# Constant matmuls in planned TensorE gaps, and longer DMA times in the planner of a hybrid decoder layer

## The chip, the cores and the metric

One core of one Trainium2 chip runs the whole program. The metric is device microseconds (us) of one execution; the time before is the median of three runs.

## What is computed

One layer of a hybrid decoder on a prompt of 2048 tokens (plus 16 meta tokens) and on 8 short sampled sequences of 4 tokens. The reference, cut down:

```python
h = rmsnorm(x, ln1_w)
p = einsum('btd,de->bte', h, w_in)          # one wide projection, 1024 -> 10384
# branch A: causal conv + SiLU on q/k/v, then the gated delta rule in chunks of 64,
#           8 heads of 128x128 state
# branch B: token shift, LoRA decays, RWKV-7 state update, 16 heads of 64x64 state
merged = sigmoid(gA) * (oA @ w_out_a) + sigmoid(gB) * (oB @ w_out_b)
x_new = x + merged @ w_out
y = rmsnorm(x_new, lnf_w)                   # and the new states of both branches
```

## The kernel before, in words

The tokens are cut into five segments of 6 or 7 chunks of 64 (368 to 448 columns). Of each segment the kernel computes the normalised, transposed input (`hHL`, a high and a low fp32r half), then twelve units: four pairs of heads of branch A (kind G) and eight of branch B (kind R), then the sixteen gate tiles, then three closing projections (kind f). A unit begins with projections (stage P, tiles `ps_p`): for each 128 columns of a weight, `proj` (L974) takes two halves of the weight, each split into `wh` and `wl`, and runs 12 fp32r matmuls on each. Then come the conv and other elementwise work, the inversion of the chunk matrices (`iM`, `iT`, `iD`, with small transfers through DRAM: `ex`, `bk`, `Dn`, `Dt`; stage M), and the recurrence over chunks (stage C, small fp32 matmuls in `ps_c`, `ps_n`, `ps_g`). An fp32 matmul shows as four rows of MATMUL and four of LDWEIGHTS in the profile, an fp32r matmul as one of each.

All of this is first recorded and not issued. `Rec.add` (L302) makes a node of each operation, and `Rec.cost` (L346) gives it a duration and a latency: for a DMA 0.07 us on its queue and 2.1 us until it has landed. `Sched.run` (L700) then simulates the five engines with these costs and so fixes the order of every engine's instructions; `replay` (L866) issues them in that order. On the chip the engines wait for each other's data by semaphores and each runs its own list strictly in order. All DMAs are issued on the one queue of SyncE (SP).

What matters for the change in the planner:

- `pick_pe` (L812) chooses the next matmul node of TensorE among the ready ones; where it has none it returns nothing, and the plan leaves TensorE idle. `clock` (L797) lets the plan run TensorE at half speed after a stretch of its own clock in which it planned under 3000 columns.
- `can` (L541), `take` (L576) and `drop` (L586) book buffers. Weight tiles (tag `w`, ten slots of 256 KB) are taken in the order of the list `worder`; a slot is free as soon as its last planned reader is done.
- PSUM has eight banks by tag: two each of `p`, `a` and `c`, one each of `n` and `g`.

Planned costs of fp32 matmuls with 128 moving columns, by the formulas of L353 to L356: 213 ns for a stationary operand of 128x128 (mode F), 134 ns for 64x128 (C), 110 ns for 128x64 (B), 86 ns for 64x64 (A). Small products are recorded in pairs or fours on different quarters of the array, and the formulas count one of such a set.

Of the kernel before, what the change touches and what calls it, by code (L numbers as in the profile page):

```python
# [16 lines left out]
C = 64  # L17
# [229 lines left out]
class Rec:  # L247
# [98 lines left out]
    def cost(s, n, e, name, a, k, outs, ins, mode):  # L346
        f = lambda x: prod(x.shape[1:])
        if e == "PE":
            n.cols += (128 if name == "transpose" else f(a[2])) * (1 if name == "transpose" or a[1].dtype == F32R else 2)
            if name == "transpose":  # L350
                n.dur += 0.107
            elif a[1].dtype == F32R:
                n.dur += (f(a[2]) / 2.4 + 14.5) / 1000  # L353
            else:
                N = f(a[2])
                n.dur += {"A": max(54, 54 + 0.5 * (N - 64)), "B": max(56, 0.86 * N), "C": max(70, 1.05 * N), "F": max(110, 4 * N / 2.4)}[mode] / 1000  # L356
            n.lat = 0.18 if a[1].dtype == F32R else 0.27
        elif e == "SP":
            o = outs[0] if outs else a[0]
            by = prod(o.shape) * 4  # L360
            last = lambda x: x.ap[-1][1] * 4 if x.ap[-1][0] == 1 else 4
            ap = [y.ap_ if isinstance(y, V) else y for y in (a[0], a[1])]
            seg = min(last(y) for y in ap)
            nd = by / max(seg, 4)
            n.kb = max(by, nd * 256)
            n.dur, n.lat = 0.07, 2.1
        else:
            N = max(f(x) for x in outs[:1] + ins[:1]) if outs else 0
            ps = any((isinstance(x, V) and x.root.psum) for x in ins)
            if e == "DVE":  # L370
                d = N / 0.96 + 160
                if name == "scalar_tensor_tensor":
                    d += 40
                if name == "tensor_tensor_scan":
                    d = 2 * N / 0.96 + 160
            elif e == "ACT":
                d = 0.82 * N + (165 if ps else 240)
            else:
                d = {"tensor_tensor": 2.35 * N + 100, "memset": 0.6 * N + 80}.get(name, 1.1 * N + 150)
            n.dur += d / 1000  # L380
            n.lat = 0.09
        if e == "PE":
            return
# [63 lines left out]
class Sched:  # L447
# [93 lines left out]
    def can(s, n):  # L541
        need = {}
        for r in n.allocs:
            k = (r.pool, r.tag)
            need[k] = need.get(k, 0) + 1
        u = n.unit
        for k, c in need.items():
            av = len(s.free[k]) - c
            if av < 0:
                return False  # L550
            if k[1] == "w":
                if not s.worder or s.worder[0] is not n:
                    return False
                continue
            if k[0].space == PSUM:
                continue
            L = u.seqs[k]
            i = u.idx[k]
            if L[i] is not n.allocs[[(r.pool, r.tag) for r in n.allocs].index(k)]:
                return False  # L560
            for v in s.active:
                if v.age > u.age:
                    break
                if k not in v.idx:
                    continue
                h, j = v.held[k], v.idx[k]
                if v is u:
                    h, j = h + c, j + c
                if max(0, v.peak[k][j] - h) > av:
                    return False  # L570
                av += h
            if u not in s.active and max(0, u.peak[k][i + c] - c) > av:
                return False
        return True
# [11 lines left out]
    def drop(s, r):  # L586
        k = (r.pool, r.tag)
        s.free[k].append(r.slot)
        if k in r.unit.held and not r.psum and r.tag != "w":
            r.unit.held[k] -= 1  # L590

# [108 lines left out]
    def run(s):  # L700
# [2 lines left out]
        E = ["PE", "DVE", "ACT", "POOL", "SP"]  # L703
        s.rdy = {e: [] for e in E}
        s.active, s.worder, s.pq, s.cur, s.infl, s.wpend = [], [], [], None, [], []
        s.lastunit, s.late = s.porder["last"], s.porder["late"]
        tfree = dict.fromkeys(E, 0.0)
        s.mode, s.burst = "F", 0
# [12 lines left out]
        while done < total:  # L721
            s.commit()
            prog = True
            while prog:
                prog = False
                for e in E:
                    if tfree[e] > s.now + 1e-9:
                        continue
                    n = s.pick_pe() if e == "PE" else s.pick(e)
                    if n is None:  # L730
                        continue
                    prog = True
                    d = n.dur
                    if e == "PE":
                        if n.mode != s.mode:
                            d += s.SWITCH
                            s.stat["sw"] += 1
                        s.clock()
                        if s.half:
                            d *= 2  # L740
                        w0, w1 = int(s.now / 3.4133), int((s.now + d) / 3.4133)
                        for w in range(w0, w1 + 1):
                            part = min((w + 1) * 3.4133, s.now + d) - max(w * 3.4133, s.now)
                            s.cols[w] = s.cols.get(w, 0) + n.cols * part / d
                        s.mode = n.mode
                        isP = n.pt is not None and len(n.ops) * 2 > PG
                        s.burst = s.burst + 1 if isP else (s.burst if n.mode == "F" else 0)
                        s.stat["P" if isP else "s"] += n.dur
                        s.stat["idle"] += s.now - max(tfree[e], 0)
                        if n.pt is not None and n is n.pt.pe[-1]:  # L750
                            s.pq.remove(n.pt)
                    else:
                        s.rdy[e].remove(n)
                    s.take(n)
                    n.started, n.start = True, s.now
                    s.on_started(n)
                    out.append(n)
                    nstart += 1
                    tfree[e] = s.now + d
                    fin = s.now + d + n.lat  # L760
                    if e == "SP":
                        dma = max(dma, s.now) + n.kb / 330e3
                        fin = max(fin, dma + n.lat)
                    c += 1
                    heapq.heappush(ev, (tfree[e], c, None))
                    c += 1
                    heapq.heappush(ev, (fin, c, n))
                    if e == "PE":
                        s.commit()
            if not ev:  # L770
                self_dump(s)
                raise RuntimeError("stuck")
            t, _, n = heapq.heappop(ev)
            s.now = max(s.now, t)
            L = [n]
            while ev and ev[0][0] <= s.now + 1e-9:
                L.append(heapq.heappop(ev)[2])
            for n in L:
                if n is None:
                    continue  # L780
                done += 1
                n.unit.left -= 1
                if n.unit.left == 0:
                    s.active.remove(n.unit)
                for r in n.roots:
                    r.left -= 1
                    if r.left == 0:
                        s.drop(r)
                for m in n.succ:
                    m.nd -= 1  # L790
                    m.rt = s.now
                    if m.nd == 0 and m.en and not (m.pt is not None and m.eng == "PE"):
                        s.rdy[m.eng].append(m)
        s.order = out
        return out

    def clock(s):  # L797
        w = int(s.now / 3.4133)
# [62 lines left out]


BCH, BMX, BVL, AGE, ZUR = 4, 16, 3.0, 0.1, 0.5


def replay(tc, rec, order):  # L866
# [11 lines left out]
class Trunk:  # L878
# [117 lines left out]
    def setup(self):  # L996
        nc, I = self.nc, self.I
        P = self.p_c
        nc.scalar.preload_act_table_set("natural_log_exp_and_others")
        self.eps = P.tile([128, 4], F32, name="eps")  # L1000
        nc.vector.memset(self.eps[:, 0:1], EPS)
        nc.vector.memset(self.eps[:, 1:2], GN_EPS)
        nc.vector.memset(self.eps[:, 2:3], 1.0)
        nc.vector.memset(self.eps[:, 3:4], -2.4260151319598084)
        self.consts = P.tile([128, CONST_ON], F32, name="consts")
        nc.sync.dma_start(self.consts[:, 0:128], I["consts"][:, 0:128])

    def g_setup(self):
        nc, I = self.nc, self.I
# [1303 lines left out]
```

## Time and profile before

| | |
|---|---|
| median of 3 runs | 4490.87 us (4485.87 to 4494.15) |
| the profiled execution | 4488.34 us, of which its span is 4486.6 us |
| mean granted clock of TensorE | 0.936 of 2.4 GHz |
| TensorE matmul busy | 4138.6 us, 92% of the span |
| VectorE, ScalarE, GpSimd busy | 2725.4, 1973.8 and 984.4 us |
| moved by DMA | 790.08 MB |

PE is the matmul row of TensorE, PEld its weight loads, DVE VectorE, ACT ScalarE, POOL GpSimd, SPq the issuing of DMAs by SyncE. Almost every instruction has line 875, that of `replay`, so groups are told apart by the names of their tiles. PEclk is the clock that TensorE was granted: 1.00 is 2.4 GHz, 0.50 is 1.2 GHz.

### The profile page before, as it was taken

The page shows a single profiled execution, that of the slowest core. Times are in us where ns is not written, and L with a number is a line of the kernel's source. Part 1 is how long each engine was busy: PE and PEld are TensorE (multiplying, and loading weights), DVE is VectorE, ACT ScalarE, POOL GpSimd, SP SyncE. Part 2 cuts the span into 40 slices and gives each one's busy share as a digit, 9 for nine tenths or more (in the row PEclk, how much of TensorE's full clock was granted, in tenths as well). Part 3 has the DMA queues.
Part 4 walks back from the last instruction along what each step waited for, and adds up shares of the span by engine and source line. Part 5 has one row for each costly group of instructions (what it writes and reads, how often), then busy time and mean ns, then how long its engine had stood idle before and what let it go on. Part 6 is the DMA issues. An engine that isn't in the chain of part 4 may idle for free. (4 is left out here: it accounts for less than half of the span.)

```text
span 4486.6 us, 91248 instructions
## 1 busy us (share of the span) xinstructions
PE 4138.6 (92%) x32684; PEld 3467.9 (77%) x32684; DVE 2725.4 (61%) x7052; ACT 1973.8 (44%) x4842; POOL 984.4 (22%) x1972
## 2 busy tenths in 40 slices
PE   6788999998999999998999999999999999989997
PEld 6677777777878788877777787878777888768776
DVE  5877766756666554556667544676654547656642
ACT  5444543434445344444444442545444434544431
POOL 3333333323122121112212121121122102211210
PEclk9887898899999899999999999999999999999998
DMA  7544665659645456754445576544446865444457
GB/s 253 179 139 139 194 222 173 193 192 306 189 130 164 126 175 214 248 175 121 138 125 150 166 238 212 178 127 144 135 135 183 258 192 174 137 122 131 142 181 241
DMA packets 660687, 790.08 MB, mean 176 GB/s; under 512 B 251105, under 2 KB 347209, under 8 KB 660234
## 3 DMA queue, kind: packets, MB, share of 16 engines
q1 hardware_dynamic: 660234, 784.25, 56.5%
q8 instruction: 259, 4.24, 0.4%
q14 instruction: 194, 1.59, 0.1%
HBM read 602.29 MB, written 180.56 MB: 174 GB/s over the span
## 5 line engine op out<-in xcount | busy, mean ns | idle before, releaser
L875 PE MATMUL ps_p<-hHL,wh 128*128 128x448 f32 (+3 forms) x7760 | 1938.3, 378 | 39.2 <-DMA wh<-wh 20.3
L875 PEld LDWEIGHTS ps_p<-hHL,wh 128*128 128x128 f32 x7760 | 1395.4, 195 | 186.6 <-issue 62.7
L875 PE MATMUL ps_p<-hHL,wl 128*128 128x448 f32 (+3 forms) x3880 | 910.1, 357 | 1.5 <-DVE wl L875 1.0
L875 PEld LDWEIGHTS ps_p<-hHL,wl 128*128 128x128 f32 x3880 | 727.8, 193 | 36.8 <-DVE wl L875 1.6
L875 POOL COPY xo<-X 64x64 f32<-64x64 f32 x528 | 177.4, 336 | 819.5 <-ACT X L875 445.2
L875 DVE TENSOR_TENSOR iT<-iM,iD 56x1 f32<-56x1 f32 (+1 forms) x900 | 293.2, 326 | 72.4 <-DMA iD<-in_consts 54.7
L875 ACT COPY raw<-ps_p 128x448 f32<-128x448 f32 (+3 forms) x285 | 144.0, 505 | 341.2 <-PE ps_p L875 316.2
L875 DVE SCALAR_TENSOR_TENSOR cv<-raw,pv,cv 128x448 f32<-128x448 f32 (+1 forms) x360 | 261.1, 725 | 37.0 <-ACT cv L875 28.1
L875 DVE TENSOR_REDUCE iD<-iT 56x1 f32<-56x1 f32 (+1 forms) x900 | 205.1, 228 | 17.6
L875 POOL TENSOR_TENSOR wl<-wr,wh 128x512 fp32r<-128x512 f32 x105 | 146.4, 1394 | 218.7 <-ACT wh L875 101.9
L875 ACT ACTIVATE X<-ps_c,dc 64x64 f32<-64x64 f32 x224 | 69.0, 309 | 266.7 <-DVE X L875 153.4
L875 ACT CAST wh<-wr 128x512 fp32r<-128x512 f32 x210 | 129.3, 616 | 114.5 <-PE ps_p L875 36.2
L875 ACT ACTIVATE X<-ps_c 64x64 f32<-64x64 f32 x264 | 54.3, 216 | 261.7 <-DVE X L875 134.9
L875 DVE SCALAR_TENSOR_TENSOR gs<-gs,gl,ps_g 128x128 f32<-128x128 f32 x264 | 84.5, 344 | 125.2 <-PE ps_g L875 86.8
L875 POOL TENSOR_TENSOR Nt<-AL,consts 64x448 f32<-64x448 f32 (+1 forms) x80 | 93.7, 1171 | 292.9 <-DVE AL L875 288.4
L875 PE MATMUL ps_p<-mhl,wh 128*128 128x448 f32 (+2 forms) x640 | 156.1, 371 | 0.6 <-DMA wh<-wh 0.4
L875 ACT ACTIVATE sig<-cv 128x448 f32<-128x448 f32 (+2 forms) x120 | 67.4, 561 | 185.6 <-DVE cv L875 184.3
L875 PE MATMUL ps_g<-gs,cv 128*64 128x128 f32 x1056 | 122.1, 307 | 25.7 <-DVE wbd L875 9.6
L875 DVE TENSOR_SCALAR X<-ps_c,dc 64x64 f32<-64x64 f32 x224 | 65.1, 291 | 128.2 <-PE ps_c L875 83.8
L875 PEld LDWEIGHTS ps_n<-Z,Wp 64*64 64x64 f32 x3168 | 113.2, 146 | 34.5 <-DVE Z L875 15.4
L875 PE MATMUL ps_n<-Z,Wp 64*64 64x16 f32 (+1 forms) x3168 | 123.1, 222 | 12.4 <-DVE Z L875 12.1
L875 DVE TENSOR_TENSOR Z<-Dt,ps_n 128x336 f32<-128x336 f32 (+1 forms) x180 | 67.0, 372 | 101.7 <-PE ps_n L875 84.2
(337 smaller groups left out, 7483.4 us busy)
## 6 DMA issues: line engine op xcount, KB each, us to landing
wh<-wh SPq DMA_DIRECT2D x1050, 256.0 KB
wl<-wl SPq DMA_DIRECT2D x1050, 256.0 KB
wr<-in_wt SPq DMA_DIRECT2D x210, 256.0 KB
gl<-gt SPq DMA_DIRECT2D x72, 224.0 KB
gt<-gt SPq DMA_DIRECT2D x48, 224.0 KB
xt<-in_x_prompt SPq DMA_DIRECT2D x29, 256.0 KB
xt<-in_x_prompt SPq DMA_DIRECT2D x13, 512.0 KB
out_y_p<-xt SPq DMA_DIRECT2D x26, 256.0 KB
```

Source lines behind the costliest of these rows:

```text
L875: getattr(getattr(nc, eng), name)(*[g(x) for x in a], **{q: g(x) for q, x in k.items()})
```

## The change

Three things change, all of them in the planner.

- Where `pick_pe` has nothing, the planned time is past 60 us and projections are still to come, `keep` may place a matmul of constants: 128 columns of `consts` against a stationary operand of `consts`, in the mode of the last matmul, written to the first free PSUM bank in the order `n`, `a`, `g`, `c`, `p`. It does so while the present stretch of the plan has under 4500 columns (it counts as 256). Nobody reads the result. The bank is booked for its duration and 0.2 us more.
- DMAs that are not loads or stores of weights count as landing after 3.0 us and not 2.1.
- A weight slot is taken again at the earliest 1.0 us after its last planned reader is done.

```diff
-            n.dur, n.lat = 0.07, 2.1
+            n.dur, n.lat = 0.07, WLAT if n.stage == "W" else DLAT
...
-                if not s.worder or s.worder[0] is not n:
+                if not s.worder or s.worder[0] is not n or (WMAR and s.freed.get(s.free[k][0], 0) > s.now - WMAR):
                     return False
...
         s.free[k].append(r.slot)
+        if r.tag == "w":
+            s.freed[r.slot] = s.now
+            if WMAR:
+                s.wake.append(s.now + WMAR + 0.001)
...
                     n = s.pick_pe() if e == "PE" else s.pick(e)
+                    if n is None and e == "PE" and s.now > KT0 and (len(s.porder["unit"]) or s.pq):
+                        n = s.keep()
...
+    def keep(s):
+
+        w = int(s.now / 3.4133)
+        if s.cols.get(w, 0) + (s.cols.get(w - 1, 0) if False else 0) >= KEEP or (w + 1) * 3.4133 - s.now < 0.2:
+            return None
+        for tag in "nagcp":
+            k = next((k for k in s.free if k[1] == tag and k[0].space == PSUM), None)
+            if k and s.free[k]:
+                break
+        else:
+            return None
+        r = Root(k[0], tag, [128, 512], F32, "keep", None)
+        r.psum, r.left = True, 1
+        r.unit = s.nounit
+        n = Node(-1, "PE", None, "P")
+        m = n.mode = s.mode
+        K, M = (64 if m in "AC" else 128), (64 if m in "AB" else 128)
+        c = s.rec.consts
+        n.ops = [("tensor", "matmul", (V(r, None, (("__getitem__", ((slice(0, M), slice(0, 128)),), {}),)), c[0:K, 0:M], c[0:K, 0:128]), dict(start=True, stop=True))]
+        n.dur = {"A": 86, "B": 110, "C": 134, "F": 213}[m] / 1000
+        n.lat, n.cols, n.roots, n.allocs = 0.2, 256, [r], [r]
+        return n
...
+WLAT, DLAT, WMAR = 2.1, 3.0, 1.0
+KEEP, KT0 = 4500, 60.0
...
+        nc.consts = self.consts
```

## Rows read from the trace of the kernel before

**Rows 1.** Cores: span and mean granted clock

```profile
core 0: 4486.6 us, clock 0.936
```

**Rows 2.** The page: TensorE's busy time, and its clock in 40 slices

```profile
PE 4138.6 (92%) x32684; PEld 3467.9 (77%) x32684; DVE 2725.4 (61%) x7052; ACT 1973.8 (44%) x4842; POOL 984.4 (22%) x1972
...
PEclk9887898899999899999999999999999999999998
```

**Rows 3.** Stretches: window, length, busy us (instructions) of PE, PEld, DVE, ACT, POOL, clock, DMA

```profile
60.00:900.00 840.00, 755.50 (x5885) 628.22 (x5887) 605.36 (x1633) 392.85 (x942) 291.74 (x538) 0.85 0.59 186
900.00:4300.00 3400.00, 3201.91 (x25692) 2682.47 (x25689) 2034.52 (x5229) 1512.37 (x3705) 659.17 (x1360) 0.96 0.56 171
4300.00:4486.60 186.60, 153.83 (x978) 133.51 (x977) 58.01 (x115) 40.05 (x107) 22.11 (x33) 0.91 0.67 220
```

**Rows 4.** Sums over the 65 stretches at clock 0.50: all instructions, then tile ps_p

```profile
sum 574.44, PE 482.35 PEld 392.26 DVE 331.91 ACT 216.22 POOL 133.66; mean PE 7.42 PEld 6.03 DVE 5.11 ACT 3.33 POOL 2.06
...
sum 574.44, PE 221.00; mean PE 3.40
```

**Rows 5.** Timeline of PE: six projection matmuls at clock 0.50, six at 1.00

```profile
2423.95 2.61 PE L875 MATMUL ps_p<-hHL,wh 128*128 128x448 f32 x6
...
2428.97 1.36 PE L875 MATMUL ps_p<-hHL,wh 128*128 128x448 f32 x6
```

**Rows 6.** Timeline of PE, three gaps: start, us, what [idle before <-releaser]

```profile
115.75 0.46 PE L875 MATMUL ps_a<-sh,onesR 128*128 128x416 f32 x1 [2.75 <-DVE sh L875]
117.92 0.71 PE L875 MATMUL ps_a<-sl,onesR 128*128 128x416 f32 x1 [1.72 <-DVE sl L875]
...
4393.25 3.33 PE L875 MATMUL ps_p<-hHL,wh 128*128 128x448 f32 x8 [16.61 <-DMA wh<-wh]
```

**Rows 7.** Waits of PE over the span: total us, times, longest

```profile
PE ps_c L875 <- DVE X L875: 39.6, 28, 6.5
PE ps_n L875 <- DMA Dn<-bk: 34.1, 23, 5.7
PE ps_p L875 <- DMA wh<-wh: 20.7, 4, 16.6
...
PE ps_n L875 <- DMA Dt<-bk: 7.3, 5, 2.6
```

**Rows 8.** A stall at 1722 us: timelines of SP, DVE and PE

```profile
1705.01 4.82 SPq L875 DMA_DIRECT2D Dn<-bk  x7
1709.87 3.72 SPq L875 DMA_DIRECT2D Dt<-bk  x8
...
1716.54 1.80 SPq L875 DMA_DIRECT2D hHL<-oA  x4
...
1721.79 0.56 DVE L875 TENSOR_TENSOR hHL<-hHL 128x384 fp32r<-128x384 f32 x1 [7.97 <-ACT hHL L875]
1722.39 0.23 DVE L875 TENSOR_SCALAR X<-ps_c 64x64 f32<-64x64 f32 x1
...
1722.68 0.49 PE L875 MATMUL ps_c<-xo,consts 128*64 128x64 f32 x4 [5.44 <-DVE X L875]
```

**Rows 9.** The chain of waits: start, us from issue to landing of single DMAs

```profile
3034.15 2.86 DMA iM<-ex
...
3295.64 6.42 DMA xt<-in_x_prompt
...
3917.61 4.55 DMA bk<-iD
...
3997.76 4.09 DMA iM<-ex
...
4032.19 3.02 DMA ex<-AL
```

**Rows 10.** Waits of all engines: total us, times, longest

```profile
DVE iM L875 <- DMA iM<-ex: 135.3, 46, 10.4
```

**Rows 11.** Waits of the DMA queue of SP: total us, times, longest

```profile
SPq L875 <- PE ps_p L875: 1270.6, 1017, 17.2
```

**Rows 12.** Timeline of PE's weight loads: two fp32 products of 128 stationary columns

```profile
636.59 0.96 PEld L875 LDWEIGHTS ps_a<-sX,KM 32*128 32x128 f32 x8 [0.23 <-issue]
```

More of the change, by code (lines that the diff above doesn't have):

```diff
@@ L705, in run @@
         s.active, s.worder, s.pq, s.cur, s.infl, s.wpend = [], [], [], None, [], []
+        s.freed, s.wake = {}, []
+        s.nounit = Unit(-1, 'k', 0)
         s.lastunit, s.late = s.porder["last"], s.porder["late"]
@@ L746, in run @@
                         isP = n.pt is not None and len(n.ops) * 2 > PG
+                        s.stat["keep"] = s.stat.get("keep", 0) + (n.unit is None) * n.dur
                         s.burst = s.burst + 1 if isP else (s.burst if n.mode == "F" else 0)
@@ L755, in run @@
                     n.started, n.start = True, s.now
-                    s.on_started(n)
+                    if n.unit is not None:
+                        s.on_started(n)
                     out.append(n)
@@ L769, in run @@
                         s.commit()
+            for x in s.wake:
+                c += 1
+                heapq.heappush(ev, (x, c, None))
+            s.wake = []
             if not ev:
@@ L779, in run @@
                 if n is None:
+                    continue
+                if n.unit is None:
+                    s.drop(n.roots[0])
                     continue
```

## The prediction

> **What bounds the kernel now.** I began with the clock of the core and the page: TensorE is granted 0.936 of 2.4 GHz and its matmuls are busy for 92% of the span [rows 1, 2], so TensorE sets the time and loses it in two ways, by gaps and by running at 1.2 GHz. Next I cut the span into stretches [rows 3]. In 60 to 900 us PE is idle for 840 - 755.5 = 84.5 us and the clock is 0.85; in 900 to 4300 us it is idle for 198 us at 0.96; after 4300 for 33 us. So the first segment is the worst by far, but most of the idle time lies behind it.
>
> What does the low clock cost? There are 65 stretches at 1.2 GHz, 574 us together, with PE busy for 482 us, of which 221 us are projections (`ps_p`) [rows 4]. Six projection matmuls take 2.61 us at 1.2 GHz and 1.36 at 2.4 [rows 5], so half of 221, some 110 us, is lost on them alone. If all that ran there were slowed to half, it would be 241 us. Small products depend more on each other than on the clock, so I take 130 us, 2.0 us for each fall.
>
> The gaps are of two kinds. At 115.75 and 117.92 us PE waits 2.75 and 1.72 us for VectorE while there is little else to do, and at 4393 us 16.6 us for the closing projections [rows 6]: a planner that knows the dependences sees such gaps. In the other kind the chip is later than the plan. At 1722 us PE stands for 5.44 us before a small product of the recurrence: VectorE sat 7.97 us before a tile of `hHL` whose loads came behind seven `Dn` and eight `Dt` transfers on SP, and the `X` that PE wanted stood behind it [rows 8]. Fifteen issues took 8.5 us there, 0.57 us each, where the planner counts 0.07. The chain shows landings of 2.86 to 4.55 us for the small transfers of the inversion and 6.42 for an input tile [rows 9], where it counts 2.1. The plan has no idle time at such places.
>
> **The longer DMA time.** It moves 0.9 us of the lateness into the plan: the consumer is placed 0.9 us later in its engine's list and something else goes ahead. PE waited directly for `Dn` 23 times and for `Dt` 5 times [rows 7]: 28 x 0.9 = 25 us at most. VectorE waited 46 times for `iM` [rows 10], 46 x 0.9 = 41 us; VectorE has slack, so I let a third reach PE, 14 us. If 12 of the falls of the clock go with these stalls, 12 x 2.0 = 24 us. Together -63 us. Bounds: nothing, if the waits only move to the next item of the same late chain, since issue time (0.57 against 0.07) is still uncounted; and -25 - 41 - 65 = -131 us if every wait shrinks and half the falls go. The cover is the projections: while a unit waits longer, PE must have another's weights at hand.
>
> Here a rule of the Trainium skill speaks against the change. DMA: Bandwidth & Descriptors, in its account of the two cost components, gives a transfer about 2.0 us fixed plus its bytes over 436 GB/s; by it the old 2.1 us is right for a small transfer and the new 3.0 only delays consumers. The trace does not agree: two `iM` loads of the same kind took 2.86 and 4.09 us [rows 9]. By the page this part would be 0 and not -63.
>
> **The margin on weight slots.** The SP queue stood 1017 times, 1271 us in all, at a weight transfer whose slot PE had not yet left [rows 11], 1.25 us each, with small transfers queued behind it. One us later in the plan takes up to 1 us off each such wait. On the other side each weight arrives later. PE waited only 20.7 us for `wh`, of which 16.6 in the closing gap [rows 7], so there are about 4 us of weight waits in the body, and ten slots are five halves of 12 matmuls, some 13 us at 2.4 GHz, where six take 1.36 us [rows 5]. I count 0, with -15 to +20 us as the ends (a quarter of the gain on VectorE's 41 us spread over PE's waits, and five times today's 4 us of weight waits). The delay also holds a slot in the first segment, where three tiles serve one half; work that hides it there is the idle time itself.
>
> **The constant matmuls.** Their price on the chip is not shown, since the kernel has none. The nearest row is two fp32 products with 128 stationary columns, one after the other on the same part of the array: eight weight loads in 0.96 us, the last of them 0.19 long, so (0.96 - 0.19)/7 = 0.11 us a pass and four passes, 0.44 us, a product [rows 12]. The planner counts 0.213 (mode F) or 0.134 (C) for the same thing, because its formulas were made for sets that share the array. With 64 stationary columns I estimate half, 0.22 us, against 0.086 or 0.110. So a planned gap that is filled takes about 2.1 times its length on the chip, more outside mode F. Bounds for one: 0.213 if successive ones with the same weights run as planned, 0.88 at 1.2 GHz.
>
> How many are there? I cannot see the plan's gaps. Lower end: the closing gap and a few more, 20 us. Upper end: all 283 us of idle time from 60 to 4300 us. I take 100 us, the 84.5 of the first segment and the end, since the stalls of the middle look unplanned. At a mean of 0.19 us that is some 530 matmuls, and at 0.4 us each 210 us of PE on the chip. They stand where PE idled for about 100 us; of the other 110 I let 60 vanish, because the chip's gaps are longer than the planned ones and because a PE that comes later waits less for late DMAs. That leaves +50. Against it the clock: 60 to 900 us holds 840 x 0.15 x 2 = 252 us at 1.2 GHz [rows 3], 252/574 x 130 = 57 us of the loss; I give two thirds of that back, 40, and 10 elsewhere. Net 0; bounds -110 (falls nearly all gone, little overrun) to +150.
>
> A product of constants must also wait until the last reader of its bank is done on the chip, in a plan that thinks it done. What is queued behind it is all of PE. I count 0, since the next real product mostly waits for the same VectorE; the end is +40 (100 such waits of 0.4 us, a small share of VectorE's lateness).
>
> **Sum.** 4488.3 (the profiled execution: span 4486.6 and 1.7 around it) - 63 + 0 + 0 + 0 = 4425. The median of the runs is 2.5 us above that execution, less than this sum can tell; I state 4427.
>
> **The rivals.**
>
> *The constants overrun (slower).* Place: PE's list, at each planned gap. If the plan has 250 us of gaps, 1300 matmuls take some 530 us in place of 250; of the 280 too many, 80 vanish in longer gaps, the clock gives back 100 of its 130, and the DMA part, with the chip now behind the plan, 50: 4488 + 200 - 150 = 4538. It decides from an unhidden overrun of about 113 us, the forecast's 63 and 50 together, that is some 470 matmuls of mode F with 0.24 too many, none hidden. For it: the price in [rows 12] is double the planned one. Against: PE is idle for 283 us in the body and the traced stalls with a late DMA are not planned ones. Chance 0.25.
>
> *Nothing to speak of.* The plan hardly idles after 900 us, few matmuls are placed, and the late chains stay as late as they are because issue time is still uncounted: 4480 to 4499. The landing rule named above would have this effect, with the consumers merely placed later. For it: at 0.57 us an issue [rows 8], eight queued transfers are 4.6 us, against the 0.9 now granted. Chance 0.10.
>
> *Clock and stalls both.* The gaps are mostly planned, the fillers keep 2.4 GHz nearly throughout (110 of 130 us), little overrun shows, and DMAs give 63: 4488 - 173 = 4315; with part of it, 4310 to 4370. Against: the falls of the middle follow stalls that the plan does not see. Chance 0.14.
>
> *Banks tie PE to VectorE.* The fillers wait for a late reader where PE would have gone on to projections: +40 and more, with the DMA gain half lost, 4488 + 40 - 30 = 4498 to 4520. Chance 0.06.
>
> **How the numbers follow.** The forecast has 0.45, with its own range 4370 to 4470 (the DMA part at both ends). A measurement of this kernel can tell about 0.2%, 9 us, from no change. Faster: 0.45 + 0.14 = 0.59; same 0.10, slower 0.25 + 0.06 = 0.31. The range 4330 to 4540 leaves out half of the double gain and the upper third of the overrun.
>
> **What the profile after would show.** Right: a clock of 0.95 to 0.97, above 0.90 in 60 to 900 us; groups of matmuls from `consts` alone, some 2000 rows (four each), with weight loads 0.11 us apart; PE's waits for `Dn` and VectorE's for `iM` down by a third; the queue's waits for `ps_p` well under 1271 us. Wrong: PE busier by over 300 us with the same idle time (the overrun); a clock still at 0.94 (the falls were not planned gaps); new waits for `wh` in the body (the margin starves PE); waits of the constant products for ScalarE or VectorE (the banks).

## The result, and the profile after

The changed kernel takes 4590.72 us (median of 4 runs, 4586.22 to 4597.94) where the kernel before took 4488.37 beside it: a ratio of 1.023, with a 95% interval of 1.0208 to 1.0251. It is slower by 2.3%. I had forecast 4427 us, 1.4% faster, and a range that ended at 4540.

One thing ahead of all that follows. The text before the prediction says that an fp32 matmul shows as four rows in the profile. It shows as two. The changed program issues 1798 constant matmuls, and they are 3596 rows. The price in my prediction, and in the expectations below the count of 899 and the prices of 0.45 and 0.35 us for a constant matmul, come from that mistake.

The cores view of the kernel after:

```profile
core 0: 4584.4 us, clock 0.978
```

Its page: TensorE's busy time, its clock in 40 slices, and the two groups of constant matmuls (`keep`), which line 917 issues (busy us, mean ns of one row | idle us before).

```profile
PE 4406.5 (96%) x36280; PEld 3757.5 (82%) x36280; DVE 2719.5 (59%) x7052; ACT 1977.4 (43%) x4842; POOL 988.4 (22%) x1972
...
PEclk9999999999999999999999999999999999999999
...
L917 PE MATMUL keep<-consts 128*128 128x128 f32 (+2 forms) x3596 | 529.9, 286 | 2.4 <-ACT sq L917 0.7
L917 PEld LDWEIGHTS keep<-consts 128*128 128x128 f32 (+2 forms) x3596 | 470.0, 163 | 22.4 <-issue 2.3
```

The change does what it says. The clock rose from 0.936 to 0.978 against [rows 1, 2], and PE's idle time fell from 4486.6 - 4138.6 = 348 us to 4584.4 - 4406.5 = 178 us. Both are what one would wish for, and the kernel is slower. PE is now busier by 268 us. That is the reading to take from these lines: a busy share of 96% says nothing about whether the work was wanted.

Two of the stretches of [rows 3] in the kernel after, in the same columns:

```profile
60.00:900.00 840.00, 807.47 (x6781) 699.34 (x6780) 578.09 (x1534) 382.00 (x904) 278.72 (x505) 0.96 0.57 181
900.00:4300.00 3400.00, 3307.74 (x27159) 2800.85 (x27159) 2006.91 (x5169) 1504.18 (x3678) 657.97 (x1352) 0.98 0.55 172
```

And the sum over its stretches at clock 0.50, as in [rows 4]:

```profile
sum 200.49, PE 181.33 PEld 155.89 DVE 107.45 ACT 55.01 POOL 31.62; mean PE 6.04 PEld 5.20 DVE 3.58 ACT 1.83 POOL 1.05
```

The time at 1.2 GHz fell from 574 to 200 us. In 60 to 900 us PE's idle time went from 84.5 to 32.5 us and the clock from 0.85 to 0.96, and yet VectorE did less work there: 578 us and 1534 instructions where it had 605 and 1633. So in the same 840 us the program came less far.

The waits that [rows 7, 10 and 11] showed, in the kernel after (total us, times, longest), first those of PE:

```profile
PE ps_c L917 <- DVE X L917: 12.9, 12, 4.8
...
PE ps_p L917 <- DMA wh<-wh: 12.6, 5, 3.3
...
PE ps_n L917 <- DMA Dt<-bk: 7.4, 8, 1.3
...
PE ps_n L917 <- DMA Dn<-bk: 0.3, 1, 0.3
```

Of all engines, and of the queue of SP:

```profile
DVE iM L917 <- DMA iM<-ex: 96.5, 30, 10.0
```

```profile
SPq L917 <- PE ps_p L917: 1110.1, 842, 19.6
```

PE's wait for `Dn` is gone (34.1 us to 0.3), VectorE's for `iM` fell from 46 to 30 times, and the queue stands less behind the projections.

What does one constant matmul cost? The groups of PE by shape in the kernel after (rows | busy us, mean ns of one row):

```profile
L917 PE MATMUL keep<-consts 128*128 128x128 f32 x1424 | 234.1, 290 | 1.3 <-DVE hHL L917 0.4 <-DVE y L917 0.4 <-DVE oa L917 0.3
L917 PE MATMUL keep<-consts 64*64 64x128 f32 x1258 | 169.3, 283 | 1.0 <-ACT sq L917 0.7 <-ACT ysq L917 0.3
L917 PE MATMUL keep<-consts 128*64 128x128 f32 x814 | 113.5, 285 | 0.0
...
L917 PE MATMUL keep<-consts 64*128 64x128 f32 x100 | 12.9, 278 | 0.1
```

Two runs of them in its timeline of PE (start, us):

```profile
4401.96 1.69 PE L917 MATMUL keep<-consts 64*64 64x128 f32 x14
...
4404.10 1.37 PE L917 MATMUL keep<-consts 128*64 128x128 f32 x11
```

Fourteen rows of the smallest shape take 1.69 us, the last of them about 0.27, so one row follows another by (1.69 - 0.27)/13 = 0.11 us, and the eleven rows of 128x64 give the same. In the trace the rows of 128x128 follow each other by 0.11 us too (a median of 112 ns at 2.4 GHz). In a row of them at 2.4 GHz a constant matmul of any shape thus takes 2 x 0.11 = 0.22 us. The planner has 0.213 for the largest, which is right, and 0.086, 0.110 and 0.134 for the others. By its prices the 712, 629, 407 and 50 matmuls are 152 + 54 + 45 + 7 = 257 us; on the chip, counted from each row's start to the next row's or to its own end, they took 432 us.

### The profile page after: what moved, and what is told of

The parts are those of the page before. It is cut to its first block, busy times and chain, and to the rows that moved or that the text cites. A ratio compares the mean times of both kernels' runs of the same rounds, so it can differ in the third digit from the quotient of the medians.

```text
span 4584.4 us, 98539 instructions
## 1 busy us (share of the span) xinstructions
PE 4406.5 (96%) x36280; PEld 3757.5 (82%) x36280; DVE 2719.5 (59%) x7052; ACT 1977.4 (43%) x4842; POOL 988.4 (22%) x1972
## 4 chain that ended last, share of the span: by engine, by line
PE 79%; DMA 7%; DVE 5%; SPq 4%; issue 2%; ACT 2%; POOL 1%; DVEq 0%; ACTq 0%; POOLq 0%
PE ps_p L917 47%; PE ps_a L917 10%; PE keep L917 8%; PE ps_c L917 5%; PE ps_g L917 5%; SPq L917 4%; PE ps_n L917 4%; DMA wl<-wl 1%; DVE cv L917 1%; DMA iM<-ex 1%; DMA wh<-wh 1%; DMA EG<-gcd 1%; DVE iT L917 1%; DMA wr<-in_wt 1%; DMA bk<-iD 1%
## 5 line engine op out<-in xcount | busy, mean ns | idle before, releaser
L917 PE MATMUL ps_p<-hHL,wh 128*128 128x448 f32 (+3 forms) x7760 | 1942.2, 374 | 22.8 <-DMA wh<-wh 12.6
L917 PEld LDWEIGHTS ps_p<-hHL,wh 128*128 128x128 f32 x7760 | 1343.2, 191 | 171.9 <-issue 59.7
L917 PE MATMUL ps_p<-hHL,wl 128*128 128x448 f32 (+3 forms) x3880 | 898.4, 354 | 1.4 <-DVE wl L917 0.8
L917 PEld LDWEIGHTS ps_p<-hHL,wl 128*128 128x128 f32 x3880 | 716.9, 190 | 35.4 <-DVE wl L917 1.1
L917 PE MATMUL keep<-consts 128*128 128x128 f32 (+2 forms) x3596 | 529.9, 286 | 2.4 <-ACT sq L917 0.7
L917 PEld LDWEIGHTS keep<-consts 128*128 128x128 f32 (+2 forms) x3596 | 470.0, 163 | 22.4 <-issue 2.3
L917 DVE SCALAR_TENSOR_TENSOR cv<-raw,pv,cv 128x448 f32<-128x448 f32 (+1 forms) x360 | 247.3, 687 | 71.6 <-ACT cv L917 64.3
L917 DVE TENSOR_SCALAR X<-ps_c 64x64 f32<-64x64 f32 x264 | 58.5, 227 | 119.0 <-PE ps_c L917 69.9
```

Of the source, the lines that this page charges most:

```text
L917: getattr(getattr(nc, eng), name)(*[g(x) for x in a], **{q: g(x) for q, x in k.items()})
```

## The experiments

The profile and the time of each kernel were taken beside runs of the kernel before on the same chip. Ratios are to the kernel before. Not all runs had the same chip: the kernel before took 4475 to 4505 us beside them. So two kernels of the table are compared by their ratios, and spans of different chips with that in mind.

| kernel | constants issued | median us | ratio, 95% interval |
|---|---|---|---|
| the change | 1798 | 4590.7 | 1.0230, 1.0208 to 1.0251 |
| its plan, constants not issued | 0 | 4496.1 | 1.0011, 0.9992 to 1.0031 |
| no constants planned | 0 | 4417.0 | 0.9834, 0.9801 to 0.9866 |
| constants alone, old DMA time, no margin | 1551 | 4597.2 | 1.0230, 1.0189 to 1.0271 |
| constants booked at 0.45 and 0.23 us | 917 | 4508.1 | 1.0031, 1.0015 to 1.0048 |
| margin alone | 0 | 4494.8 | 0.9987, 0.9969 to 1.0004 |
| longer DMA time alone | 0 | 4432.6 | 0.9837, 0.9808 to 0.9866 |
| one-pass constants, planned | 3031 | 4572.2 | 1.0163, 1.0129 to 1.0196 |
| no planned hold-up | 63 | 4455.3 | 0.9889, 0.9863 to 0.9916 |
| 350 inserted, one bank | 350 | 4447.3 | 0.9905, 0.9874 to 0.9937 |
| 938 inserted, one bank | 938 | 4760.9 | 1.0605, 1.0568 to 1.0642 |
| constants after 1200 us only | 599 | 4454.8 | 0.9920, 0.9896 to 0.9944 |
| 0.45 us for each DMA issue | 0 | 4416.6 | 0.9833, 0.9812 to 0.9854 |
| 350 inserted, banks in turn | 350 | 4408.2 | 0.9844, 0.9820 to 0.9869 |
| 938 inserted, banks in turn | 938 | 4465.6 | 0.9970, 0.9949 to 0.9991 |
| planned without a bank, not issued | 0 | 4451.8 | 0.9943, 0.9919 to 0.9966 |
| 2011 inserted, one pass | 2011 | 4486.3 | 1.0014, 0.9996 to 1.0032 |
| DMAs at 3.1 us, no constants | 0 | 4457.7 | 0.9953, 0.9936 to 0.9970 |
| 129 inserted, long gaps | 129 | 4417.2 | 0.9873, 0.9850 to 0.9896 |

### The plan, without issuing them

```diff
     for n in order:
+        if n.unit is None:
+            continue
         for r in n.allocs:
```

> The plan of the changed kernel, its order on every engine, but the 899 constant matmuls are left out when the plan is issued. They take 432 us of PE's time in the changed kernel. Theory A (their time on PE is the loss): their 432 us go, and the chip's idle time and low clock come back about as in the kernel before (170 and 165 us), so 4591 - 432 + 335 = 4494 or less, within 1% of the kernel before. Theory B (the loss is the new order, in which the recurrence lags the projections by some 90 us and the end of the program lies open): the tail stays some 100 us longer, now with PE idle in it, and the time stays at 4560 to 4590.

It gave 1.0011, with a span of 4501.3 us and a clock of 0.932. Its page, the first line of the busy times:

```profile
PE 4139.4 (92%) x32684; PEld 3456.2 (77%) x32684; DVE 2720.5 (60%) x7052; ACT 1975.0 (44%) x4842; POOL 992.0 (22%) x1972
```

The sum over its stretches at clock 0.50:

```profile
sum 611.53, PE 481.62 PEld 380.65 DVE 338.36 ACT 196.56 POOL 124.04; mean PE 8.45 PEld 6.68 DVE 5.94 ACT 3.45 POOL 2.18
```

This is the same order of all real work, so the difference to the changed kernel is what the constants do on the chip: 4584.4 - 4501.3 = 83 us in the profiled executions, 1.023/1.0011 = 2.2% by the ratios. PE's idle time falls by (4501.3 - 4139.4) - 177.9 = 184 us. The matmuls take 432. So 432 - 184 = 248 us of their time stood where PE would have worked, and the real work takes the rest, 248 - 83 = 165 us, less of PE than before. Most of that is the clock: PE was busy at 1.2 GHz for 482 us without the constants and for 181 with them. Both kernels have one order, so their real rows can be compared one by one. Rows with no gap and no constant behind them that ran at 1.2 GHz in the first and at 2.4 in the second became 136 us shorter, those the other way round 13 longer. So at least 123 of the 165 us are the clock. Some 40 more stand at rows that had a gap behind them: there a constant now begins before the row's end, so that the row is counted shorter, mostly without being so. Theory A is right for these 2.2%, though 4496 is 2 us above its 4494; the 4560 to 4590 of theory B did not come.

### No constants, and the two other edits one by one

```diff
-KEEP, KT0 = 4500, 60.0
+KEEP, KT0 = 0, 60.0
```

> No constant matmuls in the plan at all; DMAs at 3.0 us and the margin of 1.0 us on weight slots stay, and the plan is made anew. Theory A (the constant matmuls are the whole loss, and the longer DMA time gives what I predicted): 4420 to 4450. Theory B (the planner's two other edits cost, or the order does): 4500 to 4590.

0.9834: 1.7% faster than the kernel before, and 3 us below what theory A gave. No kernel of the study is clearly faster. Its span is 4415.1 us, its clock 0.948. Its page, the first line of the busy times:

```profile
PE 4098.1 (93%) x32684; PEld 3438.5 (78%) x32684; DVE 2717.6 (62%) x7052; ACT 1982.2 (45%) x4842; POOL 988.7 (22%) x1972
```

Two of its waits:

```profile
DVE iM L917 <- DMA iM<-ex: 81.1, 30, 8.6
...
PE ps_n L917 <- DMA Dn<-bk: 24.6, 26, 2.4
```

VectorE waits for `iM` 30 times and not 46, and PE's idle time is 4415.1 - 4098.1 = 317 us, 31 less than before. The margin alone, also without constants:

```diff
-WLAT, DLAT, WMAR = 2.1, 3.0, 1.0
+WLAT, DLAT, WMAR = 2.1, 2.1, 1.0
```

> No constant matmuls, DMAs at 2.1 us as before, the margin of 1.0 us on weight slots alone. The two planner edits together gave 4417 where the kernel before has 4493, some 76 us. If the longer DMA time gives it all, as I predicted (63 there, 0 for the margin), this is within 15 us of the kernel before: 4478 to 4508. If the margin gives it, 4417 to 4450.

The longer time alone, also without constants and with a margin of 0.05 us:

```diff
-WLAT, DLAT, WMAR = 2.1, 3.0, 1.0
+WLAT, DLAT, WMAR = 2.1, 3.0, 0.05
```

> No constant matmuls, DMAs at 3.0 us, and a margin of only 0.05 us on weight slots. If the longer DMA time gives the 76 us: 4410 to 4440. If the margin gives them: 4470 to 4510. If each needs the other, both this run and the margin alone stay above 4450.

The margin does nothing that can be measured (0.9987), the longer DMA time does it all (0.9837): both came where I had expected them. The other two edits undone, with the constants kept:

```diff
-WLAT, DLAT, WMAR = 2.1, 3.0, 1.0
+WLAT, DLAT, WMAR = 2.1, 2.1, 0.0
```

> The constant matmuls with DMAs at 2.1 us and no margin, as the planner before had them. Theory A: the loss stands without the other edits, and is larger by what they gave: 4590 to 4650. Theory B: if the other edits make the loss, this is near the kernel before, 4450 to 4510.

1.0230, the same loss with 1551 of them. So the constants make it without help, though here the gain of the longer DMA time does not show on top, which theory A had expected. Its time, 4597, is in the range of theory A, at its lower end.

I then gave the planner the time that the SP queue takes for an issue:

```diff
-            n.dur, n.lat = 0.07, WLAT if n.stage == "W" else DLAT
+            n.dur, n.lat = 0.45, WLAT if n.stage == "W" else DLAT
```

(with `KEEP` at 0)

> No constant matmuls, 3.0 us and 1.0 us as in the change, and 0.45 us in place of 0.07 for each DMA's time on the SP queue, about what the trace shows. If late DMAs still cost PE because the plan leaves out the issue time, another 20 to 80 us go: 4340 to 4400. If the 3.0 us already stood for it, no change from the plan without constant matmuls, 4400 to 4430, or slower if the queue becomes what bounds the plan.

0.9833, no change. The issue time that I thought was still owed gave nothing. And yet the waits fell: in this run VectorE waits for `iM` 15 times, 21 us in all, where it was 30 times and 81 us, and PE for `Dn` 6.9 us where it was 24.6. Shorter waits for small transfers did not by themselves make the kernel faster.

### How far a plan scatters

```diff
-WLAT, DLAT, WMAR = 2.1, 3.0, 1.0
+WLAT, DLAT, WMAR = 2.1, 3.1, 1.0
```

(with `KEEP` at 0)

> No constant matmuls, margin 1.0 us, DMAs at 3.1 us in place of 3.0: a plan that differs from the one without constant matmuls by nothing that should matter. It shows how far the time moves with the plan alone: within 0.3% of 0.983 if order effects of 1 to 2% have a cause of their own, up to 1% off if any change of the plan scatters so far.

0.9953 where 3.0 us gave 0.9834. A tenth of a microsecond in one planning constant moves the time by 1.2%. This is one pair of plans, and three others, with 3.0 us and a different margin or issue time, lie within 0.9833 to 0.9837; so how widely plans scatter is not known. But a difference of about 1% between two plans can come without a cause that one could name; a difference between kernels that keep one order cannot be put down to the plan.

### Constants put into a fixed order

To keep the order, I made the plan without constants and put them into PE's list afterwards, ahead of each real matmul before which this plan has a gap, as many as fit at a given price. `KEEP` is 0 for the plan, and the limit by columns in `keep` is left out. The first run has prices of 0.45 us (128 stationary columns) and 0.23 (64), the second those of the change.

```diff
+                    was = s.was = s.mode
...
+                    if e == "PE" and s.now > KT0 and (len(s.porder["unit"]) or s.pq):
+                        for _ in range(int((s.now - tfree[e]) * 1000 / {"A": 230, "B": 230, "C": 450, "F": 450}[was])):
+                            x = s.keep()
+                            if x is not None:
+                                x.roots[0].slot = s.free[(x.roots[0].pool, x.roots[0].tag)][0]
+                                out.append(x)
                     s.take(n)
```

> The plan without constant matmuls (DMAs at 3.0 us, margin 1.0 us), its order of all real work kept exactly; 350 constant matmuls are put into PE's list afterwards, where that plan leaves PE idle, as many as fit at 0.45 and 0.23 us. If the loss came from the planning (real work held up and reordered in the plan), this is not slower than the plan without them, 0.983 of the kernel before, and the clock gives something: 0.970 to 0.985. If constant matmuls cost on the chip wherever they stand: 350 at some 0.35 us are 120 us of PE, and the time is 0.990 to 1.010 of the kernel before.

> The same with as many as fit at the prices of the change (0.213, 0.134, 0.110, 0.086 us): 938 in place of 350, in the same gaps. If the underpriced number is what hurts on the chip, this is above the run with 350 by up to 588 x 0.3 = 180 us, less what idle time takes up: I expect 60 to 120 us more than there. If it is the planning that hurts, both are the same within 20 us.

0.9905 and 1.0605, the second with an average clock of 0.937 in spite of 938 constants. It is 314 us above the first, where I had expected 60 to 120. Here I had made a new wait. Whose it is, the waits of PE's weight loads say, in the run with 350 and in that with 938:

```profile
PEld keep L919 <- PE keep L919: 62.3, 206, 0.5
```

```profile
PEld keep L919 <- PE keep L919: 248.1, 748, 0.5
```

All went to the first free bank, and each waited some 0.33 us (248.1/748) for the one before it in that bank. In the changed kernel this costs 2 us, since its plan books the bank a little longer than the matmul and so moves to the next. With another free bank each time:

```diff
-                                x.roots[0].slot = s.free[(x.roots[0].pool, x.roots[0].tag)][0]
+                                F = sorted(((k[1], q, k) for k in s.free if k[0].space == PSUM for q in s.free[k]), key=lambda f: f[:2])
+                                s.rot = getattr(s, "rot", -1) + 1
+                                x.roots[0].tag, x.roots[0].slot = F[s.rot % len(F)][:2]
```

> As the run with 350 constant matmuls inserted into the plan without them, but each goes to another free bank than the one before it; there, 206 of them waited 62 us for the constant matmul before them in the same bank. If that wait made the 0.7% by which that run lay above the plan without them: 0.975 to 0.985 of the kernel before. If their time on PE made it: 0.987 to 0.993, unchanged.

> As the run with 938 inserted, with another free bank each time; there they waited 248 us for each other, and it took 1.0605. If they cost what their passes take on PE (938 at about 0.35 us are 330 us, less some 100 us of idle time and some 60 us of the low clock): 1.010 to 1.035 of the kernel before, like the changed kernel. If the planning makes its loss: 0.980 to 1.000.

0.9844 with 350 and 0.9970 with 938, in the same order as the plan without constants at 0.9834. The second is below the 1.010 to 1.035 that I gave if their time on PE made the loss of the change, and in the range that I gave if planning them did. But I had counted 330 us for the 938, and they took 245; 85 us less moves the first range to 0.991 to 1.016. So it does not speak against their time. The run with 350 has a span of 4408.9 us and a clock of 0.960, that with 938 one of 4486.4 us and 0.962. The lines of their pages, that with 350 first:

```profile
PE 4143.1 (94%) x33384; PEld 3481.5 (79%) x33384; DVE 2722.8 (62%) x7052; ACT 1982.9 (45%) x4842; POOL 992.0 (22%) x1972
```

```profile
PE 4263.2 (95%) x34560; PEld 3608.4 (80%) x34560; DVE 2718.9 (61%) x7052; ACT 1983.4 (44%) x4842; POOL 986.2 (22%) x1972
```

The sum is made as above. The 938 took 245 us of PE, counted from row to row. PE's idle time fell from 317 to 4486.4 - 4263.2 = 223 us, so 94 of the 245 us filled idle time of the chip and 151 did not. The real work took 80 us less, and 71 are the loss of 4486.4 - 4415.1. With 350 they took 105 us, 51 of them in idle time, and the real work took 60 less: about even. (These are spans of two chips; by the ratios 938 lose 1.4%, some 60 us, and 350 nothing.) Compared row by row as above, at least 39 of the 60 us and 53 of the 80 are the clock. So the first third brings three quarters of what 938 bring in these two executions; the profiled one of the 938 is the slowest of its ten, and over all runs the clock rises from 0.946 to 0.960 and to 0.968, which makes it two thirds. The rest costs its time and brings little.

Then matmuls of one pass, with fp32r constants (`nc.consts` is set in `g_setup`, behind the copy into `bocm`):

```diff
-        nc.consts = self.consts
...
+        nc.consts = self.bocm
...
-                        for _ in range(int((s.now - tfree[e]) * 1000 / {"A": 230, "B": 230, "C": 450, "F": 450}[was])):
+                        for _ in range(int((s.now - tfree[e]) * 1000 / {"A": 60, "B": 60, "C": 112, "F": 112}[was])):
```

> Constants of type fp32r, one pass each, 2011 of them inserted at 0.112 and 0.060 us into the idle time of the plan without them, order kept, banks in turn. If the fault is only price and order, these fill the same gaps at the right length: PE is not held up, the clock rises above 0.96, and the time is 0.965 to 0.980. If filling a planned gap costs on the chip whatever the price, since the chip is not idle where the plan is: 0.990 to 1.020.

And the fp32 constants again, only in the long gaps. The price was meant to fill half of each; it does so with 128 columns, but the 53 of 64 columns, booked at 0.114 us, take twice that and nearly fill theirs:

```diff
-                        for _ in range(int((s.now - tfree[e]) * 1000 / {"A": 230, "B": 230, "C": 450, "F": 450}[was])):
+                        for _ in range(int((s.now - tfree[e]) * 500 / {"A": 114, "B": 114, "C": 220, "F": 220}[was]) if s.now - tfree[e] > 1.0 else 0):
```

> The order without constant matmuls kept, 129 of them inserted, banks in turn, only into gaps of the plan over 1.0 us and only for half of the gap. With 350 in all gaps the clock gained what their time cost (0.984). If long planned gaps are gaps of the chip too, the clock gains most of that and their time costs less: 0.975 to 0.982. If not: 0.983 to 0.987.

1.0014 and 0.9873. One-pass matmuls that fill the gaps to the end cost as much as the others (they took 203 us of PE, counted from row to row), so the price of one is not the point: filling the planned gaps of this order to their end costs, with either kind. Even 129 in long gaps alone are no gain over none.

### Constants planned in other ways

```diff
-        n.dur = {"A": 86, "B": 110, "C": 134, "F": 213}[m] / 1000
+        n.dur = {"A": 230, "B": 230, "C": 450, "F": 450}[m] / 1000
```

> The changed kernel, with the constant matmuls booked in the plan at 0.45 us for 128 stationary columns and 0.23 us for 64, as the chip shows them, in place of 0.213, 0.134, 0.110 and 0.086. Theory A (they overrun because the plan books them at a third to a half of their time): about half as many are placed, what they take on PE is in the plan, and the time falls to 4480 to 4540. Theory B (order): 4560 to 4600, with the tail as long as in the changed kernel.

1.0031 with 917 of them. The price was not the true one, as I now know: right for the two shapes of 64 columns, double for the two of 128. Half as many cost about 2% less than 1798, as theory A had it, but still 2% more than none.

```diff
-        n.dur = {"A": 86, "B": 110, "C": 134, "F": 213}[m] / 1000
-        n.lat, n.cols, n.roots, n.allocs = 0.2, 256, [r], [r]
+        n.dur = {"A": 60, "B": 60, "C": 112, "F": 112}[m] / 1000
+        n.lat, n.cols, n.roots, n.allocs = 0.2, 128, [r], [r]
```

(with the fp32r constants)

> The changed kernel with constants of type fp32r, which make one pass and not four, booked at 0.112 us (128 stationary columns) and 0.060 us (64), and counted as 128 columns. Theory A (too much time of PE for each): what they take falls from 432 us to under half of that, with the clock still above 0.96 if their activity counts, and the time lands at 4430 to 4510. If what costs is rather that they are planned at all, as the 79 us between the plan not issued and the one without them suggest, the time stays at 4500 to 4560.

1.0163, with 3031 of them. That is above both ranges, by 12 us above the second. Nor was the condition of theory A met: the planner placed so many more that they took 336 us of PE, counted from row to row, and not under half of 432.

```diff
                         n = s.keep()
+                        if n is not None and ev and ev[0][0] < s.now + n.dur:
+                            n = None
```

(with the booked times of 0.45 and 0.23 us)

> The changed kernel with constant matmuls booked at 0.45 and 0.23 us, and placed only where no event of the plan falls within that time, so that none holds up a real instruction in the plan. If the 79 us of the order come from such hold-ups, the order is as good as the one without constant matmuls, few of them are placed, and the time is 4400 to 4440. If a constant matmul costs on the chip even where the plan has nothing else, 4460 to 4520.

0.9889 with only 63 left, 4455 us and so between the two ranges. From 0.983 it differs by less than the two plans above do, so it decides nothing.

```diff
-KEEP, KT0 = 4500, 60.0
+KEEP, KT0 = 4500, 1200.0
```

> The changed kernel, but constant matmuls are planned only after 1200 us of the plan, so none in the first segment. The recurrence falls behind there: in the changed kernel the small products of the recurrence reach 20% of their number 83 us later than in the kernel before, and stay so. If that lag makes the loss, this is 4430 to 4490; if the loss is made all along, 4530 to 4580.

0.9920. Leaving out the first 1200 us leaves 599 of the 1798 constants and takes 3.1% of the time away, more than the 1.2% above. The time is in the range that I gave to a lag of the recurrence in the first segment. But two thirds of the constants are gone too, and three quarters of the loss against none (0.9% is left of 4.0%). So it is not shown that the place matters and not the number.

The last one books PE's time but no bank and issues nothing: `n.roots` and `n.allocs` stay empty, and the search for a free bank is left out.

> The plan of the changed kernel with constant matmuls that take PE's time in the plan and no bank, and are not issued. The plan with bank and time, not issued, took 1.001 where the plan without constant matmuls takes 0.983. If the booked banks spoil the order, this is 0.980 to 0.990; if PE's time in the plan does (a real matmul that comes ready has to wait for the end of a constant one), 0.995 to 1.005.

0.9943, between the two. With 1.2% between two plans above it decides nothing on the banks.

## Why the prediction was wrong

**The constant matmuls are the step that failed**, where I had net 0. They cost 4.0% against the plan without them, some 175 us: 2.2% by being issued at the same order, and 1.8% by the other order that the planner makes when it books them. Three terms of the step were mis-sized, and a fourth, the order, was not in the sum.

*How many.* I took 100 us of planned gaps, the idle time of the first segment and the end, and 530 matmuls. The plan books 257 us of them, 1798 matmuls. My argument was that the stalls of the middle are not in the plan. That may be so, but it does not follow that the plan has few gaps. The planner of the kernel before, by its own count, leaves PE idle for 198 us where `keep` may act, 121 of them after 900 us; without constants, but with the two other edits, it is 198 again. Nor are they simply filled: the changed plan books 257 us and still has 84 idle. By its own clock it loses 7 us to half speed and not 110, and it ends 46 us later than the plan without constants.

*Price.* I took 0.44 us for 128 stationary columns and half for 64, from [rows 12], where I read eight rows as two products; they are four. The true price is 0.22 us for every shape. The mean that I used, 0.4, was nearly twice too high, and the count more than three times too low; 210 us of PE's time became 432.

*What it covers.* I let 160 of 210 us vanish in idle time and slack, three quarters. The plan without issue shows 184 of 432, and the fixed order 94 of 245 and 51 of 105: about 40 to 50%. The premise of the change fails here: where the plan has PE idle, the chip often has work. I take it that PE on the chip is behind the plan, so that by then the data are there; no run shows this. The clock, for its part, gave more than I allowed: 123 us at the least against 50, about the 130 that I thought it could give in all. It is the main reason why 248 us of displaced work cost 83 to 95.

*The signs.* Nearly all that I had named as signs of being right came: a clock of 0.978 (I had 0.95 to 0.97), 0.96 in 60 to 900 us, weight rows 0.11 us apart, shorter waits for `Dn`, `iM` and `ps_p`. My sign for the overrun did not: PE is busier by 268 us and not by over 300, and its idle time is not the same but half. None of these signs weighed the fillers' time against what it brought.

**The longer DMA time** was right in direction, and in size as far as it can be told: I had -63 us, and the plan with it and without constants is 4415 against 4487 in the profiled executions, -71. But 3.1 us in place of 3.0 gives 0.5% and not 1.7, so a part of it may be luck. The parts of the sum are not borne out one by one: PE's wait for `Dn` fell by 10 us and came 26 times in place of 23, its idle time fell by 31 us where I had 39, and its busy time fell by 40, where I had 24 for the clock. And the run with the issue time cut the waits further and gained nothing. Why the longer time helps is thus not shown. In all four plans with 3.0 us or more and no constants planned for (0.9834, 0.9837, 0.9833 and 0.9953) the kernel is faster than before. DMA: Bandwidth & Descriptors in the Trainium skill, in its two cost components, would have made 2.1 us right and this part nothing; its fit is for transfers that GpSimd issues, where here SP does. These four runs do not bear that out.

**The margin** was costed at 0, and it is 0.9987. The weights did not come late: PE's wait for `wh` is 12.6 us in the changed kernel.

**The banks.** A wait of a constant matmul for a late reader, which I had at 0, hardly shows: 2.4 us before all of them and 22.4 before their weight loads, of which no single releaser makes more than 2.3. As a wait on the chip that rival is out; whether booked banks spoil the order is open (below).

**The rival that came true** is the overrun, with 0.25. Its place and its sign were right (250 us of planned gaps, 530 us of PE, 4538), and its sum is nearer to what happened than the forecast: 257 us and 432. That it came so near is in part luck: 1798 matmuls at 0.22 us took the place of 1300 at 0.4, and the time is still 53 us above its 4538. What I gave for it, the doubled price, was wrong; that the chip is not idle where the plan is, I had noted only on the side of the stalls.

**What is not settled.** From 0.9834 (no constants) to 1.0230 there are 4.0%. Issuing them costs 2.2% at a fixed order, which is shown. The other 1.8% lies in the order that the planner makes when it books them. Two plans that differ by 0.1 us in one constant are 1.2% apart, so this may be a cost of the booking, of the banks, or chance. In the changed kernel the end lies open, and constants fill it (PE busy with `keep`, out of 50 us each):

```profile
4350.00:4400.00 50.00, 0.00 (x0) 0.00 (x0) 0.90 0.44 134
4400.00:4450.00 50.00, 31.18 (x251) 26.88 (x252) 1.00 0.07 18
4450.00:4500.00 50.00, 32.75 (x239) 30.81 (x237) 1.00 0.59 196
```

The recurrence (`ps_c`) of the last units is late there. Its last row in the kernel before, in the changed one, and in its plan without the constants issued (timeline of PE):

```profile
4369.88 0.34 PE L875 MATMUL ps_c<-AY,X 128*64 128x64 f32 x4
```

```profile
4450.82 0.34 PE L917 MATMUL ps_c<-AY,X 128*64 128x64 f32 x4
```

```profile
4386.29 0.48 PE L919 MATMUL ps_c<-AY,X 128*64 128x64 f32 x4
```

That is 81 us later than before, of the 98 by which the span is longer. In the plan without the constants issued it is 16, so most of the lateness comes with issuing them and not with the order.

## What to carry to other kernels

Filler work that a planner puts into its own idle time is free only where the chip is idle at the same place of the engine's list; here it was for 40 to 50% of the filler's time. Put fillers into a fixed order and take the sum (filler's time, idle time gone, clock gained) before you let them change the plan, and stop early: the first third of them brought two thirds to three quarters of the clock's gain. And measure what a meaningless change of the plan does before giving a 1% difference between two plans a cause.

## What the runs showed of the hardware

Consecutive fp32 matmuls of 64 stationary columns on the same part of the array, with 128 moving columns, follow each other at the same 0.11 us a row as those of 128, at 2.4 GHz. I had estimated half. With the fp32r constants, which make one row each, it is different (timeline of PE in the run with 2011):

```profile
813.63 1.90 PE L921 MATMUL keep<-bocm 64*64 64x128 f32 x28 [0.23 <-ACT gt L921]
...
4354.40 14.17 PE L921 MATMUL keep<-bocm 128*128 128x128 f32 x125 [0.65 <-DVE gl L921]
```

Taking off the last row, 0.22 and 0.27 us, these are 0.062 us a row for 64 stationary columns and 0.112 for 128. TensorE: Matmul & The Clock Gate in the Trainium skill, under LDWEIGHTS, gives the stationary columns divided by 1.2 in ns, 53 for 64 columns and 107 for 128. The fp32r rows are near that at both shapes; the fp32 rows do not show the saving. What sets their 0.11 us was not tested.

Consecutive matmuls that nobody reads, each starting a new group in the same bank, waited for one another in this program, 0.33 us each; in different banks they did not.

A clock of 0.978 and a PE at 96% can go with a slower kernel: with 0.948 and 93% the same work took 0.9834 of the time before, and not 1.0230.
